# Who makes the low halves of the experts' weights: twelve subtractions moved from GpSimd to VectorE in a hybrid encoder block

## The chip, the cores and the metric

One core of one Trainium2 chip runs the whole block in one launch. The metric is the device time of a launch in microseconds (us). Engines are named as the profile names them: PE is TensorE, PEld its weight loads, DVE is VectorE, ACT is ScalarE, POOL is GpSimd, and SP is SyncE, which here only issues transfers.

## What is computed

The block is an encoder layer on 2048 tokens of 1024 numbers: a projection, differential attention, a Hyena long convolution, a gated merge, and then a mixture of 16 experts in which each expert chooses 256 tokens. Only the last part is touched:

```
g, idx = lax.top_k(aff.transpose(0, 2, 1), cap)
xin = jax.vmap(lambda ub, ib: ub[ib])(u, idx)
hg = jnp.einsum('becd,edf->becf', xin, w_gate)
hu = jnp.einsum('becd,edf->becf', xin, w_up)
eo = jnp.einsum('becf,efd->becd', jax.nn.silu(hg) * hu, w_down)
```

The weighted rows of `eo` are then added back to the tokens they came from.

## The kernel before

**Two-part numbers.** Each float32 operand of a matmul is kept as a high part `hi` (a rounded copy) and a low part `lo`, the operand minus `hi`. A product takes three matmuls: high with high, high with low, low with high. The helper `split` (L40 to L43) has ACT write `hi` (L42) and DVE write `lo` (L43), and it is used all over the kernel.

**The experts.** `moe_phase` handles the experts one after another. For expert e, `hidden(e)` takes eight weight tiles in the order gate 0, up 0, gate 1, up 1 and so on; a tile is 128x2048 numbers, 1 MB. `down(e)` takes four more. Between the two, `turn(e + 1)` transposes the tokens gathered for the next expert on PE (L1554) and splits them. Each weight tile goes through `weight`: a transfer from SP's queue into a buffer `r` (L1504, or L1501 for the down weights; three buffers), then `hi` into `wh` and `lo` into `wl` (four buffers each). So the transfer of a tile waits until the split of the tile three places before it is done, and ACT's copy waits until PE is through with the tile four places before.

**The two kinds of experts.** For the first three experts (`ALONE = 3`) the gate and up matmuls take 256 columns each (L1590); for the others a different arrangement of 512 and 256 columns is used (L1615, L1618). Only for the first three, `weight` is called with `early` for four of the twelve tiles: the up tiles of j = 2 and 3, and the down tiles of j = 1 and 3. There ACT writes `hi` (L1508) and GpSimd, not VectorE, writes `lo` (L1509).

**What else runs there.** While PE works for the first experts, DVE also looks for the 256 best tokens of the following ones: `narrow` for experts 1 and 2 (a search whose counts go through PE, L1310 to L1333, then L1352 to L1377), and `narrow_all` for all the others at once (L1389 to L1405). `onehot` (L1521) and `index` (L1528 on PE, L1533 to L1538 on DVE) turn the result into row numbers, with which GpSimd gathers the tokens by an indirect transfer (L1541). GpSimd also issues the indirect transfers that add an expert's result to the output (L1641). After each group of matmuls `step()` advances this search.

**What sets the order.** Each engine runs its instructions in the order of its own queue. That order is made when the program is built, by a scheduler that places instructions by estimated times, so that a change of engine for one instruction can move others.

Of the kernel before, what the change touches and what calls it, by code (L numbers as in the profile page):

```python
# [9 lines left out]
F32 = mybir.dt.float32  # L10
# [3 lines left out]
AF = mybir.ActivationFunctionType  # L14
ALU = mybir.AluOpType
# [16 lines left out]
def dap(ap, off, dims):  # L32
    return bass.AP(tensor=ap.tensor, offset=ap.offset + off, ap=dims)
# [6 lines left out]
def split(nc, hi, lo, src):  # L40

    nc.scalar.activation(hi, src, AF.Copy)  # L42
    return nc.vector.tensor_tensor(lo, src, hi.bitcast(F32), ALU.subtract)  # L43


def mm3(nc, out, a, b, start, stop):

    nc.tensor.matmul(out, a[0], b[0], start=start, stop=False)  # L48
    nc.tensor.matmul(out, a[0], b[1], start=False, stop=False)  # L49
    return nc.tensor.matmul(out, a[1], b[0], start=False, stop=stop)  # L50
# [1213 lines left out]
ALONE = 3  # L1264
# [214 lines left out]
def moe_phase(E, aff, u2d, wg, wu, wd, out):  # L1479
    nc, tc = E.nc, E.tc  # L1480
    rows = out.rearrange("b l d -> (b l) d")
    with ExitStack() as ctx:
# [9 lines left out]

        READY = {}

        def weight(w, e, j, down, early=False):
            if (w is wu, e, j, down) in READY:
                return READY.pop((w is wu, e, j, down))
            r = pr.tile([128, 2048], F32, name="r")
            if down:
                v = r.rearrange("p (k c) -> p k c", c=1024)  # L1500
                nc.sync.dma_start(v, dap(w, (e * FH + j * 256) * D, [[D, 128], [128 * D, 2], [1, D]]))  # L1501
            else:
                v = r.rearrange("p (k c) -> p k c", c=256)
                nc.sync.dma_start(v, dap(w, e * D * FH + j * 256, [[FH, 128], [128 * FH, KD], [1, 256]]))  # L1504
            hi = pw.tile([128, 2048], F32R, name="wh")
            lo = pw.tile([128, 2048], F32R, name="wl")
            if early:
                nc.scalar.activation(hi, r, AF.Copy)  # L1508
                nc.gpsimd.tensor_tensor(lo, r, hi.bitcast(F32), ALU.subtract)  # L1509
            else:  # L1510
                split(nc, hi, lo, r)
            c = 1024 if down else 256
            return hi.rearrange("p (k c) -> p k c", c=c), lo.rearrange("p (k c) -> p k c", c=c)

# [59 lines left out]
        def hidden(e):  # L1574
            x2 = XT[e]
            hh = ph.tile([128, 8, CAP], F32R, name="hh")
            hl = ph.tile([128, 8, CAP], F32R, name="hl")
            for j in range(4):
                s = po.tile([128, 2, CAP], F32, name="s")
                if e < ALONE:  # L1580
                    ps = []
                    for w in (wg, wu):
                        wt = weight(w, e, j, False, j > 1 and w is wu)
                        p = sg.tile([128, 2, CAP], F32, name="pg")
                        for f in range(2):
                            cs = slice(f * 128, (f + 1) * 128)
                            for a in range(2):
                                for k in range(KD):
                                    for b in range(2 - a):
                                        nc.tensor.matmul(p[:, f], wt[a][:, k, cs], x2[:, k, b], start=a + k + b == 0,  # L1590
                                                         stop=a == 1 and k == KD - 1)
                            step()
                        ps.append(p)
                    nc.scalar.activation(s, ps[0], AF.Silu)
                    nc.vector.tensor_tensor(s, s, ps[1], ALU.mult)
                else:
                    gu = []
                    for w in (wg, wu):
                        wt = weight(w, e, j, False)
                        o = s if w is wg else po.tile([128, 2, CAP], F32, name="su")  # L1600
                        for f in range(2):
                            beside(o[:, f], wt, x2, f)
                            step()
                        gu.append(o)
                    nc.scalar.activation(s, s, AF.Silu)
                    nc.vector.tensor_tensor(s, s, gu[1], ALU.mult)
                split(nc, hh[:, 2 * j:2 * j + 2], hl[:, 2 * j:2 * j + 2], s)
            HT[e] = hh, hl

        def beside(o, wt, x2, f):  # L1610

            p = sg.tile([128, 2, CAP], F32, name="pg")
            cs = slice(f * 128, (f + 1) * 128)
            for k in range(KD):
                nc.tensor.matmul(p.rearrange("p a c -> p (a c)"), wt[0][:, k, cs],  # L1615
                                 x2[:, k].rearrange("p a c -> p (a c)"),
                                 start=k == 0, stop=False, skip_group_check=True)
                nc.tensor.matmul(p[:, 0], wt[1][:, k, cs], x2[:, k, 0],  # L1618
                                 start=False, stop=k == KD - 1, skip_group_check=True)
            nc.scalar.activation(o, p[:, 1], AF.Copy)  # L1620
            nc.vector.tensor_tensor(o, o, p[:, 0], ALU.add)

        def down(e):
            hh, hl = HT[e]
            ix, g, _ = IX[e]
            ys = [sy.tile([128, 512], F32, name="py") for _ in range(4)]
            for j in range(4):
                wt = weight(wd, e, j, True, e < ALONE and j % 2 == 1)
                for f in range(2):
                    k = j * 2 + f  # L1630
                    for s in range(2):
                        for c in range(2):
                            mm3(nc, ys[s * 2 + c], (hh[:, k, s * 128:(s + 1) * 128], hl[:, k, s * 128:(s + 1) * 128]),
                                (wt[0][:, f, c * 512:(c + 1) * 512], wt[1][:, f, c * 512:(c + 1) * 512]),
                                k == 0, k == 7)
                    step()
            for s in range(2):
                y = po.tile([128, D], F32, name="y")
                for c in range(2):
                    nc.scalar.activation(y[:, c * 512:(c + 1) * 512], ys[s * 2 + c], AF.Copy, scale=g[:, s:s + 1])  # L1640
                nc.gpsimd.indirect_dma_start(out=rows, out_offset=bass.IndirectOffsetOnAxis(ap=ix[:, s:s + 1], axis=0),  # L1641
                                             in_=y, in_offset=None, compute_op=ALU.add)
# [16 lines left out]
        def step():  # L1659
            next(ahead, None)  # L1660
            if tick[0] >= 16:
                next(wide, None)
            tick[0] += 1
# [4 lines left out]
        for e in range(NE):  # L1668
            hidden(e)
            if e + 1 < NE:  # L1670
                turn(e + 1)
            down(e)
# [65 lines left out]
```

## Time and profile before

| | us |
|---|---|
| median of 3 runs | 3774.24 (3770.49 to 3776.69) |
| the profiled execution, its time | 3763.67 |
| the profiled execution, its span | 3761.9 |

The span runs from the first to the last instruction that the profiler saw; 1.8 us of the execution's time lie around it. In the trace, times are us from the span's start. A row of the order of time (the timeline) merges equal instructions that follow each other; its first number is the start, its second the time from the first start to the last end, and in brackets stands how long the engine sat idle before it and what ended that. [...]

### The profile page before, as it was taken

To read this page: it belongs to the slowest core of one execution; us is meant where nothing else is said; L and a number is where in the kernel's file an instruction comes from. 1 tells how busy PE (TensorE), PEld (TensorE's weight loads), DVE (VectorE), ACT (ScalarE), POOL (GpSimd) and SP (SyncE) were. 2 spreads that over 40 slices of the span, in tenths; PEclk is the share of its full clock that TensorE was granted. 3 is DMA by queue.
4 is the path that set the end of the run, shared out by engine and by line. 5 is a ranking of instruction groups with operands and counts; after the bars stand their busy time and mean duration, and the time that the engine had idled before them with its cause. 6 is when DMAs were issued, how large, how long until landed. Compare 5 with 4: busy or idle time off the path is not lost. (4 is left out here: it accounts for less than half of the span.)

```text
span 3761.9 us, 55714 instructions
## 1 busy us (share of the span) xinstructions
PE 3621.2 (96%) x21122; PEld 3128.0 (83%) x21122; DVE 2495.9 (66%) x5447; ACT 1819.1 (48%) x2787; POOL 476.8 (13%) x435
## 2 busy tenths in 40 slices
PE   8999999999999999999999799997899999999998
PEld 6788888788888888798999688886888888888887
DVE  8944552698989897167777644558775666665663
ACT  5411111566666675367666432323345555555553
POOL 0000000000000000354453100001330101100100
PEclk9999999999999999999999799998999999999999
DMA  4286774312222222766876853325556766766764
GB/s 156 76 254 165 187 188 129 115 64 84 92 83 93 64 92 71 235 176 211 237 210 202 262 165 129 108 80 168 168 179 192 220 215 205 222 208 206 224 202 123
DMA packets 449713, 607.28 MB, mean 161 GB/s; under 512 B 37467, under 2 KB 333411, under 8 KB 442789
## 3 DMA queue, kind: packets, MB, share of 16 engines
q1 hardware_dynamic: 389301, 438.81, 37.3%
q0 software_dynamic: 34736, 127.16, 12.6%
q10 hardware_dynamic: 25408, 37.76, 2.8%
q8 instruction: 166, 2.72, 0.3%
q14 instruction: 102, 0.84, 0.1%
HBM read 464.16 MB, written 139.46 MB: 160 GB/s over the span
## 5 line engine op out<-in xcount | busy, mean ns | idle before, releaser
L43 DVE TENSOR_TENSOR wl<-r,wh 128x2048 fp32r<-128x2048 f32 (+1 forms) x236 | 449.5, 1910 | 330.9 <-ACT wh L42 330.7
L1615 PE MATMUL pg<-x,wh 128*128 128x512 f32 x1664 | 587.0, 398 | 0.0
L42 ACT ACTIVATE wh<-r 128x2048 fp32r<-128x2048 f32 (+1 forms) x236 | 379.4, 1610 | 356.8 <-PE pg L1615 138.5
L1618 PE MATMUL pg<-x,wl 128*128 128x256 f32 x1664 | 466.3, 280 | 0.0
L1615 PEld LDWEIGHTS pg<-x,wh 128*128 128x128 f32 x1664 | 312.4, 188 | 75.3
L411 DVE TENSOR_SCALAR_CACHE_REDUCE x<-p 128x512 f32<-128x512 f32 x512 | 335.0, 685 | 23.4 <-PE p L410 22.8
L410 PE MATMUL p<-k,qT 128*128 128x512 f32 x1024 | 327.0, 415 | 0.0
L1618 PEld LDWEIGHTS pg<-x,wl 128*128 128x128 f32 x1664 | 314.1, 189 | 0.5
L418 ACT ACTIVATE x<-x,sm 128x2048 f32<-128x2048 f32 x128 | 256.7, 2006 | 45.8 <-DVE sm L415 42.1
L42 ACT ACTIVATE ah<-pt 128x512 fp32r<-128x512 f32 x256 | 150.1, 595 | 151.5 <-PE pt L433 150.9
L49 PE MATMUL py<-wl,hh 128*128 128x512 f32 x512 | 205.3, 401 | 0.0
L48 PE MATMUL p<-wh,uh 128*128 128x512 f32 x512 | 203.5, 398 | 0.4 <-ACT uh L134 0.4
L48 PE MATMUL py<-wh,hh 128*128 128x512 f32 x512 | 203.4, 397 | 0.0
L50 PE MATMUL py<-wh,hl 128*128 128x512 f32 x512 | 202.1, 395 | 0.0
L43 DVE TENSOR_TENSOR bl<-p,bh 128x512 fp32r<-128x512 f32 x192 | 124.7, 685 | 115.7 <-ACT bh L42 114.6
L43 DVE TENSOR_TENSOR al<-pt,ah 128x512 fp32r<-128x512 f32 x256 | 174.9, 685 | 38.8 <-ACT ah L42 37.5
L50 PE MATMUL p<-wh,ul 128*128 128x512 f32 x512 | 200.4, 392 | 0.0
L49 PE MATMUL p<-wl,uh 128*128 128x512 f32 x512 | 200.3, 392 | 0.0
L410 PEld LDWEIGHTS p<-k,qT 128*128 128x128 f32 x1024 | 171.4, 190 | 24.3 <-ACT qT L368 2.8
L1641 POOL DMA_INDIRECT out_dram<-y,ix x32 | 71.7, 2242 | 752.1 <-ACT y L1640 648.6
L433 PE MATMUL pt<-idf,x 128*128 128x128 f32 x1024 | 164.7, 272 | 0.0
L48 PE MATMUL gp<-gh,gu 128*128 128x512 f32 x384 | 157.1, 409 | 3.7 <-ACT go L294 2.4
(435 smaller groups left out, 9504.0 us busy)
## 6 DMA issues: line engine op xcount, KB each, us to landing
r<-in_w_gate SPq DMA_DIRECT2D x64, 1024.0 KB, 5.1
r<-in_w_up SPq DMA_DIRECT2D x64, 1024.0 KB, 5.7
r<-in_w_down SPq DMA_DIRECT2D x64, 1024.0 KB, 5.8
gu<-s_ud POOLq DMA_DIRECT2D x48, 1024.0 KB, 6.0
tg<-in_tg POOLq DMA_DIRECT2D x68, 384.0 KB, 4.1
xt<-in_x SPq DMA_DIRECT2D x32, 512.0 KB, 5.0
s_filt<-fo SPq DMA_DIRECT2D x128, 128.0 KB, 3.2
zr<-s_filt SPq DMA_DIRECT2D x64, 256.0 KB, 3.2
```

Of the source, the lines that this page charges most:

```text
L42: nc.scalar.activation(hi, src, AF.Copy)
L43: return nc.vector.tensor_tensor(lo, src, hi.bitcast(F32), ALU.subtract)
L48: nc.tensor.matmul(out, a[0], b[0], start=start, stop=False)
L49: nc.tensor.matmul(out, a[0], b[1], start=False, stop=False)
L50: return nc.tensor.matmul(out, a[1], b[0], start=False, stop=stop)
L410: nc.tensor.matmul(p, qT[:, t * 2 + m, a], k2[:, m, o:o + 512], start=a == 0, stop=a == 1)
L411: nc.vector.tensor_scalar(x[:, o:o + 512], p, 0.125, None, ALU.mult, ALU.max, accum_out=sm[:, c * 2 + i:c * 2 + i + 1])
L418: nc.scalar.activation(x, x, AF.Exp, bias=sm[:, 8 + m:9 + m], accum_out=acc)
L433: nc.tensor.transpose(p[:, i, t * 128:(t + 1) * 128], EX[u, t, 0][:, (g * 2 + i) * 128:(g * 2 + i + 1) * 128], E.idf)
L1615: nc.tensor.matmul(p.rearrange("p a c -> p (a c)"), wt[0][:, k, cs], x2[:, k].rearrange("p a c -> p (a c)"), start=k == 0, stop=False, ski ...
L1618: nc.tensor.matmul(p[:, 0], wt[1][:, k, cs], x2[:, k, 0], start=False, stop=k == KD - 1, skip_group_check=True)
L1641: nc.gpsimd.indirect_dma_start(out=rows, out_offset=bass.IndirectOffsetOnAxis(ap=ix[:, s:s + 1], axis=0), in_=y, in_offset=None, compute_o ...
```

## The change

`weight` loses its parameter `early`; every weight tile goes through `split`. Twelve subtractions, four for each of the first three experts, leave GpSimd's queue and stand in VectorE's.

```
-        def weight(w, e, j, down, early=False):
+        def weight(w, e, j, down):
...
-            if early:
-                nc.scalar.activation(hi, r, AF.Copy)
-                nc.gpsimd.tensor_tensor(lo, r, hi.bitcast(F32), ALU.subtract)
-            else:
-                split(nc, hi, lo, r)
+            split(nc, hi, lo, r)
...
-                        wt = weight(w, e, j, False, j > 1 and w is wu)
+                        wt = weight(w, e, j, False)
...
-                wt = weight(wd, e, j, True, e < ALONE and j % 2 == 1)
+                wt = weight(wd, e, j, True)
```

Lines behind L1507 have a number lower by 4 in the changed kernel: L1590 is L1586 there, L1595 is L1591, L1541 is L1537, L1641 is L1637. The scheduler also moves other instructions. Three places show how.

POOL, from the gather for the first expert on, before:

```order
L1541 DMA xg<-s_u,ix 128x1024 x2
L1509 TENSOR_TENSOR wl<-r,wh 128x2048 x2
L1541 DMA xg<-s_u,ix 128x1024 x2
L1509 TENSOR_TENSOR wl<-r,wh 128x2048 x2
L1641 DMA out_dram<-y,ix 2048x1024
L1541 DMA xg<-s_u,ix 128x1024 x2
L1641 DMA out_dram<-y,ix 2048x1024
L1509 TENSOR_TENSOR wl<-r,wh 128x2048 x4
```

POOL at the same place, now:

```order
L1537 DMA xg<-s_u,ix 128x1024 x4
L1637 DMA out_dram<-y,ix 2048x1024 x2
L1537 DMA xg<-s_u,ix 128x1024 x2
L1637 DMA out_dram<-y,ix 2048x1024 x2
L1537 DMA xg<-s_u,ix 128x1024 x2
```

Only the issues of indirect transfers are left in this queue (`xg` are gathered tokens, `y` an expert's result).

DVE, in the search for the tokens of expert 1, while PE works on the gate and up tiles of expert 0 (`cnt`, `k`, `thr`, `ti`, `run` belong to the search; `wl` is a weight tile's low part), before:

```order
L1314 TENSOR_REDUCE cnt<-ge 128x15 x2
L1324 TENSOR_SCALAR k<-pt 128x15
L1333 SCALAR_TENSOR_TENSOR ti<-k,thr 128x1
L1352 TENSOR_TENSOR ti<-ti 128x1
L1356 TENSOR_SCALAR run_26318<-aff,ti 128x16
L1357 TENSOR_SCALAR run_26318<-aff,ti 128x16
L1359 COPY flag<-run_26318 128x32
```

DVE at the same place, now:

```order
L1314 TENSOR_REDUCE cnt<-ge 128x15 x2
L43 TENSOR_TENSOR wl<-r,wh 128x2048
L1324 TENSOR_SCALAR k<-pt 128x15
L1591 TENSOR_TENSOR s<-s,pg 128x512
L1333 SCALAR_TENSOR_TENSOR ti<-k,thr 128x1
L43 TENSOR_TENSOR wl<-r,wh 128x2048
L1352 TENSOR_TENSOR ti<-ti 128x1
L43 TENSOR_TENSOR hl<-s,hh 128x512
L1356 TENSOR_SCALAR run_26318<-aff,ti 128x16
L1357 TENSOR_SCALAR run_26318<-aff,ti 128x16
L1359 COPY flag<-run_26318 128x32
```

Two weight tiles' low parts and two pieces of the hidden activations (`s`, `hl`) now stand inside the search.

PE at that place (L1317 is the matmul that sums `cnt`, L1365 the first that needs `run`), before:

```order
L1590 MATMUL pg<-x_26262,wl 128x256 x7
L1317 LDWEIGHTS onesb
L1317 MATMUL pt<-cnt,onesb 128x15
L1590 MATMUL pg<-x_26262,wl 128x256
L1590 MATMUL pg<-x_26262,wh 128x256 x15
L1365 LDWEIGHTS onesb
L1365 MATMUL pt<-run_26318,onesb 128x1
```

PE at the same place, now:

```order
L1586 MATMUL pg<-x_26262,wl 128x256
L1317 LDWEIGHTS onesb
L1317 MATMUL pt<-cnt,onesb 128x15
L1586 MATMUL pg<-x_26262,wl 128x256 x7
L1586 MATMUL pg<-x_26262,wh 128x256 x16
L1586 MATMUL pg<-x_26262,wl 128x256 x8
L1586 MATMUL pg<-x_26262,wh 128x256 x16
L1586 MATMUL pg<-x_26262,wl 128x256 x8
L1586 MATMUL pg<-x_26262,wh 128x256 x6
L1365 LDWEIGHTS onesb
L1365 MATMUL pt<-run_26318,onesb 128x1
```

Between the two small matmuls stood 16 of the expert's; now there are 61.

## Rows read from the trace of the kernel before

**Rows 1.** The page: span of the profiled execution.

```profile
span 3761.9 us, 55714 instructions
```

**Rows 2.** Windows: length, busy us of PE, PEld, DVE, ACT, POOL, PEclk, DMA share, GB/s.

```profile
2600.00:2840.00 240.00, 213.75 (x1478) 195.04 (x1477) 179.42 (x410) 85.48 (x76) 74.20 (x22) 0.94 0.54 171
2900.00:3000.00 100.00, 100.00 (x556) 85.11 (x555) 59.53 (x71) 52.53 (x61) 10.57 (x6) 1.00 0.68 207
```

**Rows 3.** The order of time on PE, 2600 to 2840: its idle times.

```profile
2607.30 0.17 PE L1317 MATMUL pt<-cnt,onesb 128*128 128x15 bf16 x1 [3.70 <-DVE cnt L1314]
2618.30 0.20 PE L1528 MATMUL pt<-val,oh 128*128 128x5 bf16 x2 [3.22 <-DVE oh L1521]
2641.39 0.16 PE L1317 MATMUL pt<-cnt,onesb 128*128 128x3 bf16 x1 [3.72 <-DVE cnt L1314]
2659.07 0.66 PE L1554 MATMUL pt<-idf,xg 128*128 128x128 f32 x4 [3.95 <-DVE x L43]
...
2703.10 0.38 PE L1394 MATMUL pt<-wcnt,same 128*128 128x3 f32 x2 [1.25 <-DVE junk L1389]
2716.08 0.39 PE L1394 MATMUL pt<-wcnt,same 128*128 128x3 f32 x2 [0.77 <-DVE junk L1389]
2729.54 0.39 PE L1394 MATMUL pt<-wcnt,same 128*128 128x3 f32 x2 [1.24 <-DVE junk L1389]
...
2743.53 1.12 PE L1554 MATMUL pt<-idf,xg 128*128 128x128 f32 x4 [4.09 <-DVE x L43]
2822.42 0.66 PE L1554 MATMUL pt<-idf,xg 128*128 128x128 f32 x4 [3.90 <-DVE x L43]
```

**Rows 4.** The order of time on DVE, the same stretch.

```profile
2597.92 0.17 DVE L1327 SCALAR_TENSOR_TENSOR cand<-k,base 128x15 f32<-128x15 f32 x1
...
2598.07 0.68 DVE L43 TENSOR_TENSOR hl<-s,hh 128x512 fp32r<-128x512 f32 x1
...
2599.44 2.28 DVE L43 TENSOR_TENSOR wl<-r,wh 128x2048 fp32r<-128x2048 f32 x1
...
2601.85 4.32 DVE L1327 SCALAR_TENSOR_TENSOR cand<-k,base 128x15 f32<-128x15 f32 x1
...
2635.92 3.98 DVE L1333 SCALAR_TENSOR_TENSOR t<-k,thr 128x1 f32<-128x1 f32 x1
...
2817.15 4.61 DVE L43 TENSOR_TENSOR hl<-s,hh 128x512 fp32r<-128x512 f32 x1 [0.80 <-ACT hh L42]
```

**Rows 5.** The order of time on POOL, the same stretch.

```profile
2599.75 6.39 POOL L1509 TENSOR_TENSOR wl<-r,wh 128x2048 fp32r<-128x2048 f32 x1 [25.65 <-ACT wh L1508]
...
2635.34 4.54 POOL L1509 TENSOR_TENSOR wl<-r,wh 128x2048 fp32r<-128x2048 f32 x1 [5.49 <-ACT wh L1508]
...
2816.68 4.54 POOL L1509 TENSOR_TENSOR wl<-r,wh 128x2048 fp32r<-128x2048 f32 x1 [6.89 <-ACT wh L1508]
```

**Rows 6.** Groups of POOL's instructions: count, busy us, mean ns, idle before.

```profile
L1509 POOL TENSOR_TENSOR wl<-r,wh 128x2048 fp32r<-128x2048 f32 x12 | 57.0, 4751 | 99.8 <-ACT wh L1508 97.9 <-DVE wthr L1405 1.9
```

**Rows 7.** The order of time on PE at two granted clocks.

```profile
2643.60 1.91 PE L1590 MATMUL pg<-x,wl 128*128 128x256 f32 x8
...
2647.67 1.12 PE L1590 MATMUL pg<-x,wl 128*128 128x256 f32 x8
2648.63 0.18 PE L1317 MATMUL pt<-cnt,onesb 128*128 128x15 bf16 x1
```

**Rows 8.** The order of time on ACT: a copy that waited for its load.

```profile
2611.37 1.91 ACT L1508 ACTIVATE wh<-r 128x2048 fp32r<-128x2048 f32 x1 [6.28 <-DMA r<-in_w_up]
```

**Rows 9.** Transfers, 2575 to 2850: totals, then issues with median us to landing.

```profile
DMA packets 33093, 47.46 MB, mean 173 GB/s; under 512 B 816, under 2 KB 28464, under 8 KB 33074
...
r<-in_w_up SPq DMA_DIRECT2D x14, 1024.0 KB, 5.2
```

**Rows 10.** The order of time on POOL: two gathers.

```profile
2685.52 0.99 POOL L1541 DMA_INDIRECT xg<-s_u,ix  x1 [0.30 <-DVE junk L1389]
2686.81 2.84 POOL L1541 DMA_INDIRECT xg<-s_u,ix  x1 [0.30 <-issue]
```

## The prediction

> **What bounds the kernel now.** I read the windows first. Over the stretch of the first three experts, 2600 to 2840 us, PE is busy 213.75 of 240 us at a mean granted clock of 0.94; later, from 2900 to 3000, it is busy all the time at 1.00, with DVE at 60% and the transfers at 207 GB/s [rows 2]. So the end of the kernel is set by PE alone, and a microsecond that PE loses before 2840 is a microsecond of the span of 3761.9 us [rows 1]. The stretch has 26.25 us in which PE does nothing, and a further price in clock.
>
> The second view is the order of time on PE. Nine idle times make 25.84 of those 26.25 us (3.70, 3.22, 3.72, 3.95, 1.25, 0.77, 1.24, 4.09, 3.90), and every one was ended by DVE: by the counts of the search, the one-hot rows, or the low part of the turned tokens [rows 3]. So the question is why DVE was late. It was not short of time as such: it is busy 179 of 240 us.
>
> The third view, the order of time on DVE, answers that. The same kind of instruction that takes 0.17 us at 2597.92 takes 4.32 us at 2601.85; a piece of hidden activation takes 0.68 us at 2598.07 and 4.61 at 2817.15 [rows 4]. There are twelve such long rows in the stretch, the shortest 3.98 us. The fourth view, the order of time on POOL, shows twelve subtractions L1509, 57.0 us in all [rows 5, 6]. They match one to one, and a pair ends together: POOL's first runs from 2599.75 to 2606.14 and DVE's long row ends at 2606.17; POOL's at 2635.34 ends at 2639.88, DVE's at 2639.90 [rows 4, 5]. POOL's first row is itself 6.39 instead of 4.54 us long, and the 1.85 us of difference are nearly the 1.97 us for which DVE's subtraction, begun at 2599.44, still ran. So the two engines do not do these things side by side: whichever comes second stands still until the first is done. A subtraction on POOL costs DVE some 4 us, in place of the 2.28 us that it takes on DVE [rows 4].
>
> **The change, part by part.**
>
> *Twelve subtractions leave POOL.* DVE's twelve long rows go back to their own lengths of 0.2 to 0.7 us: about 12 x 4.0 = 48 us of DVE time. With them go the idle times of PE that they made, 25.8 us.
>
> *The clock.* After an idle time PE restarts at half clock: at 2643.60 eight matmuls took 1.91 us, at 2647.67 the same eight 1.12 us [rows 7]. A mean of 0.94 over 240 us is 14.4 us of full-speed work lost (13.2 to 15.6 by the rounding of the row). Some of the low clock falls into the idle time itself, where it costs nothing, so I take 13. Bounds: 0 if the clock falls for another reason, 15.6 if all of it comes back.
>
> *Twelve subtractions come to DVE.* 12 x 2.28 = 27.4 us. DVE's work in the stretch becomes 179.4 - 48 + 27.4 = 159 us, in a stretch that shrinks to about 204 us: 78%, after 75% now. It is more room than it looks, since DVE serves its queue in order and no row holds it for 4 us any more. In the later stretch DVE makes every low part by itself and PE never waits [rows 2].
>
> *The new order.* What can go wrong is a subtraction that stands in front of a row that PE needs. I take the place shown above. Behind the count DVE now has two weight subtractions, two rows of 0.68 and some ten short rows of 0.17: 4.56 + 1.36 + 1.7 = 7.6 us. PE has 61 matmuls there, and at 0.12 us each (eight from 2647.67 to 2648.63 [rows 7]) they cover 7.3 us, where the 16 before would have covered 1.9. The wait left is 0.3 us. That holds if the weights are there. The second of those two subtractions is the eighth tile's; its load starts when the fifth tile's low part is done, 2601.72 [rows 4], lands 5.2 us later [rows 9], and ACT's copy of 1.91 us [rows 8] has it ready at 2608.8. DVE gets there after two subtractions, ten short rows and one of 0.68, at 2608.7. So that row is in time, but with nothing to spare. For all twelve I take 12 x 0.25 = 3 us of new waits; the bounds are 0 and 27.4 us, if every added subtraction came between PE and what it waits for.
>
> *The other queues.* SP's loads lose a wait: a buffer `r` that POOL released after 4.5 us or more is released by DVE after 2.28. POOL's gathers and scatters no longer queue behind subtractions. An added subtraction on DVE can still stretch one of them: a gather's issue took 2.84 us at 2686.81 beside a DVE subtraction, the one before it 0.99 [rows 10]. I cost this at nothing, because the tokens are gathered long before PE turns them; without that cover it would be 1.9 us for each expert. ACT's copies stay as they are, L42 in place of L1508.
>
> *The loads.* The stretch moves 47.46 MB in 275 us, 173 GB/s [rows 9]. With 36 us less that is 199 GB/s, below the 207 that the later stretch sustains with PE never waiting [rows 2]. So the loads do not take the gain back.
>
> *The sum.* 25.8 + 13 - 3 = 36 us. The profiled execution took 3763.67 us, its span and 1.8 us around it; it would take 3727.7. The median of the runs shown is 10.6 us above it, so I take the 36 us off the median of 3774.24: **3738 us**, 0.95% faster. A measurement of this kernel can tell about 0.2%, 7.5 us, from no change.
>
> **The rivals.**
>
> *The clock dips at the transposes anyway.* Three of the six long idle times come right before transposes (L1554) [rows 3], so these rows cannot tell whether the wait or the transposes let the clock fall there. If it was the transposes, about half of the 13 us stays: 25.8 + 6.5 - 3 = 29 us, 3745. Against it: at the restart after the first and the third idle time the rows are ordinary matmuls, and the clock was low there too [rows 7]. Chance 0.06. [...]
>
> *Part of it comes back.* The idle times go, but some of the added subtractions stand in PE's way, and the clock falls at these places. For it: the eighth tile above has no slack. With no gain in clock and 6 us of new waits it is 25.8 - 6 = 20 us: 3754. Against it: the order was made anew with the rows in it. Chance 0.11.
>
> *PE is not the only bound.* If the loads or ACT's copies held the stretch to its present length, the idle times would only move: 3774. Against it stand the 173 GB/s, under what the later stretch moves, and ACT busy 85 of 240 us. For it, one copy waited 6.28 us for its load [rows 8]. Chance 0.04.
>
> *Slower: the wait moves into DVE's queue.* POOL now sits 97.9 us waiting for ACT's copies before its twelve rows [rows 6], and nobody minds, since nothing that PE needs stands behind them. If the order puts the added rows too early, DVE takes this wait, with the search, the one-hots and the turned tokens behind it. The place is each of the twelve rows in the first three experts. It decides from (25.8 + 13) / 12 = 3.2 us of PE's time for each row; with 5 us, still below the 6.28 us that ACT's copy waited [rows 8], it is 60 - 39 = 21 us slower: 3795. Against it: at the place that I followed the row comes when its weights do. A second way to the slower side: if the long rows on DVE had another cause than POOL, the 27.4 us would only be added, 3802; the common ends speak against that. [...] Chance 0.05.
>
> *The change doesn't do what it says.* In POOL's order no subtraction is left, so this is excluded.
>
> **How the numbers follow.** The forecast has 0.74. Its own range is 30 to 41 us of gain, 41 being the whole idle time and the upper bound of the clock: 3733 to 3744. The range given must leave out no more than 2 in 10, so it takes in the first two rivals and some microseconds between executions: 3728 to 3755. Faster by over 0.2%: the forecast and the first two rivals, exactly 0.91; same: the third rival and a little of the fourth, 0.05; slower: the rest of the fourth, 0.04.
>
> **What would show it.** In the profile of the changed kernel no L1509 is left on POOL; no small DVE row in that stretch lasts over 1 us; the rows of the twelve additional L43 take 2.28 us; PE's idle time from 2600 to the start of the fourth expert falls from 26 to under 5 us, and the mean clock there rises to 0.98 or more; the fourth expert starts some 36 us earlier and everything behind it is unchanged. I am wrong if PE's idle times come back under other names: "DVE wl L43", or a search row whose DVE predecessor waited for ACT's copy.

## The result, and the profile after

The changed kernel takes **3735.26 us** (median of 4 runs, 3732.43 to 3740.06), the kernel before, run beside it on the same chip, 3775.47 (4 runs, 3770.49 to 3777.73). The ratio is 0.9897, 95% interval 0.9879 to 0.9914: 32 to 46 us faster, 40 between the medians. The forecast was 3738. The execution that was profiled took 3733.82 us.

The page of the changed kernel, beside [rows 1]:

```profile
span 3732.0 us, 55713 instructions
```

Its windows (columns as in [rows 2]; the first row answers to the first there, the second to the later stretch):

```profile
2600.00:2840.00 240.00, 238.62 (x1732) 217.18 (x1732) 182.38 (x477) 107.89 (x99) 20.52 (x14) 1.00 0.65 207
...
2900.00:3000.00 100.00, 100.00 (x599) 85.74 (x598) 66.85 (x104) 53.39 (x65) 7.79 (x6) 1.00 0.68 215
```

In the same 240 us PE now does 1732 matmuls where it did 1478, is busy 238.62 us where it was 213.75, and its granted clock (PEclk, as a share of the full one) is 1.00 where it was 0.94 [rows 2]. The order of time on PE, 2600 to 2815, has four rows with more than 0.1 us of idle time left, where before there were the nine of [rows 3] and one of 0.21 us:

```profile
2621.08 0.16 PE L1365 MATMUL pt<-run,onesb 128*128 128x1 bf16 x1 [0.19 <-DVE run L1361]
...
2670.72 0.35 PE L1394 MATMUL pt<-wcnt,same 128*128 128x3 f32 x2 [0.34 <-DVE junk L1389]
...
2692.18 0.38 PE L1394 MATMUL pt<-wcnt,same 128*128 128x3 f32 x2 [0.26 <-DVE junk L1389]
...
2699.74 0.39 PE L1394 MATMUL pt<-wcnt,same 128*128 128x3 f32 x2 [0.27 <-DVE junk L1389]
```

They sum to 1.06 us, against 25.84 for the nine. The turns, which cost 3.95, 4.09 and 3.90, have none. The order of time on DVE shows why: the small row that took 4.32 us takes 0.17 again, the piece of hidden activation that took 4.61 takes 0.68 (compare [rows 4]).

```profile
2605.61 0.17 DVE L1327 SCALAR_TENSOR_TENSOR cand<-k,base 128x15 f32<-128x15 f32 x1
...
2605.76 0.68 DVE L43 TENSOR_TENSOR hl<-s,hh 128x512 fp32r<-128x512 f32 x1
...
2616.85 2.29 DVE L43 TENSOR_TENSOR wl<-r,wh 128x2048 fp32r<-128x2048 f32 x1 [0.71 <-ACT wh L42]
```

The last row is the low part of the eighth tile, one of the twelve that came from GpSimd; it has a short wait for ACT's copy before it.

To compare the stretch itself, I take it from the first weight load for a gate or up matmul of the first expert to the first one of the fourth expert, and from there to the last one of the last expert:

| us | before | changed | difference |
|---|---|---|---|
| first three experts | 2581.4 to 2844.5, 263.1 | 2589.1 to 2814.6, 225.5 | -37.6 |
| fourth expert on | 2844.5 to 3724.4, 879.9 | 2814.6 to 3694.4, 879.8 | -0.1 |

The windows of the first row, before and then now:

```profile
2581.40:2844.50 263.10, 236.84 (x1640) 217.22 (x1639) 197.97 (x448) 97.30 (x86) 74.44 (x22) 0.94 0.55 172
```

```profile
2589.10:2814.60 225.50, 224.12 (x1642) 206.00 (x1641) 176.20 (x460) 97.21 (x86) 14.69 (x11) 0.99 0.63 201
```

PE's idle time falls from 26.3 to 1.4 us, and its busy time for the same matmuls by 12.7 (a record or two are missing).

In this execution the first expert started 7.7 us later than in that of before, in a part that the change leaves alone (every engine runs its instructions in the same order there); in the profiled executions of the first five experiments, which leave that part alone too, the start lies anywhere from 2582.1 to 2601.5. That is why the two spans differ by 29.9 us only. The gain itself is all in the stretch.

### The profile page after: what moved, and what is told of

It is laid out like the page before. It is cut to its first block, busy times and chain, and to the rows that moved or that the text cites. A ratio compares the mean times of both kernels' runs of the same rounds, so it can differ in the third digit from the quotient of the medians.

```text
span 3732.0 us, 55713 instructions
## 1 busy us (share of the span) xinstructions
PE 3610.1 (97%) x21122; PEld 3118.8 (84%) x21122; DVE 2473.9 (66%) x5459; ACT 1820.0 (49%) x2787; POOL 415.3 (11%) x423
## 5 line engine op out<-in xcount | busy, mean ns | idle before, releaser
L43 DVE TENSOR_TENSOR wl<-r,wh 128x2048 fp32r<-128x2048 f32 (+1 forms) x248 | 477.0, 1928 | 333.5 <-ACT wh L42 333.3
L42 ACT ACTIVATE wh<-r 128x2048 fp32r<-128x2048 f32 (+1 forms) x248 | 402.3, 1624 | 379.7 <-PE pg L1611 138.4
L1637 POOL DMA_INDIRECT out_dram<-y,ix x32 | 70.4, 2199 | 807.2 <-ACT y L1636 698.4
```

## Experiments

**The two halves of the change.** In the kernel before, only the down tiles' subtractions go to DVE (`hidden_pool`), or only the up tiles' (`down_pool`).

```
-                wt = weight(wd, e, j, True, e < ALONE and j % 2 == 1)
+                wt = weight(wd, e, j, True)
```

> Half of the change: the six low parts of down tiles go to VectorE, the six of up tiles stay on GpSimd. Theory (a GpSimd subtraction holds VectorE up for 4 us, and PE stands idle where something that it needs waits behind): the idle times that go with the up tiles' rows stay, 3.70 + 3.22 + 1.25 + 0.77 = 8.9 us, with about 6 us of clock behind them; so some 15 us above the changed kernel's 3735, near 3750. Rival (the low part itself came too late from GpSimd, 4.6 us in place of 2.3): PE has no idle time before a weight's low part in either kernel, so both halves would be worth nothing and the gain would come from the new order alone, 3735 or 3775. Rival (transposes let the clock fall anyway): the clock dips at the turns stay here though the down tiles are on VectorE.

```
-                        wt = weight(w, e, j, False, j > 1 and w is wu)
+                        wt = weight(w, e, j, False)
```

> The other half: the six low parts of up tiles go to VectorE, the six of down tiles stay on GpSimd. Theory: the idle times that go with the down tiles' rows stay, 3.72 + 3.95 + 1.24 + 4.09 + 3.90 = 16.9 us, with about 7 us of clock behind them; some 24 us above the changed kernel, near 3759, and the two halves together make the whole, 40 us. Rivals: as for the other half, 3735 or 3775; if the transposes let the clock fall, the dips are the same in both halves.

Measured: `hidden_pool` 3750.69 us (ratio to before 0.9942, 0.9921 to 0.9964), stretch 241.2 us; `down_pool` 3754.37 (0.9944, 0.9922 to 0.9966), stretch 244.4 us. The first has the forecast time, the second is a little better than that. Their gains, 22 and 21 us by the ratios, make 43 together, the whole change 39; each is uncertain by some 8 us. The order of time on PE shows that each half has its own waits. In `hidden_pool` the long ones are in the search and the one-hot rows, none before a transpose:

```profile
2607.83 0.17 PE L1317 MATMUL pt<-cnt,onesb 128*128 128x15 bf16 x1 [3.70 <-DVE cnt L1314]
...
2618.89 0.20 PE L1528 MATMUL pt<-val,oh 128*128 128x5 bf16 x2 [3.27 <-DVE oh L1521]
```

In `down_pool` the longest stand before two turns and at one place of the search (two of 1.25 and 1.47 us stand at other places of it):

```profile
2651.17 0.17 PE L1317 MATMUL pt<-cnt,onesb 128*128 128x15 bf16 x1 [4.16 <-DVE cnt L1314]
...
2735.86 0.66 PE L1554 MATMUL pt<-idf,xg 128*128 128x128 f32 x4 [4.09 <-DVE x L43]
...
2814.09 0.66 PE L1554 MATMUL pt<-idf,xg 128*128 128x128 f32 x4 [3.90 <-DVE x L43]
```

So the subtractions of the hidden part delayed the search, and those of the down part the turns and, here and there, the search. The clock follows the waits and not the transposes: in `hidden_pool` it is 1.00 over all three turns,

```profile
2645.00:2823.00 178.00, 175.15 (x1236) 158.50 (x1235) 136.49 (x326) 76.06 (x68) 34.79 (x12) 1.00 0.61 190
```

while in `down_pool` matmuls of 512 columns take 0.63 us soon after the two waits before turns (from 2737.16 and 2815.57 on), where they otherwise take 0.39.

**Is it GpSimd's reading?** The theory says that GpSimd holds DVE up while it reads. The rivals say that the low parts came late from it (4.6 us in place of 2.28), that its buffers came free late, or that the order of the queues was worse. So I leave the changed kernel as it is, and give GpSimd twelve instructions whose result nobody uses, at the places of the old ones. A copy of one column on ACT makes each wait for the tile's high part.

```
+        jk = pc.tile([128, 2048], F32, name="jk")
+        nc.vector.memset(jk, 0.0)
...
+            if e < ALONE and (j % 2 == 1 if down else j > 1 and w is wu):
+                nc.scalar.activation(jk[:, 0:1], hi[:, 0:1].bitcast(F32), AF.Copy)
+                nc.gpsimd.tensor_tensor(jk, jk, jk, ALU.subtract)
```

In `junk_two_reads` it is the subtraction shown; in `junk_no_read` the last line is `nc.gpsimd.memset(jk, 0.0)`, in `junk_one_read` it is `nc.gpsimd.tensor_copy(jk, jk)`.

> The changed kernel, and beside each of the twelve moved subtractions GpSimd does a useless one on a tile of its own (two inputs in SBUF, 128x2048), started by a one-column copy on ACT. Nobody waits for it, and no weight buffer is held by it. Theory (the two engines exclude each other): VectorE's long rows of 4 us are back, twelve of them, while VectorE also has its 27 us of subtractions; the whole gain is lost and some more, 3775 to 3800. Rivals (the low parts were late; the weight buffers were released late; the order was worse): none of these is touched, so it stays at 3735.

> The same, but GpSimd's useless instruction only writes (a memset of 128x2048). Theory in its narrow form (it is the reading of two inputs that excludes): no long rows on VectorE, 3735 to 3740. In a wide form (any GpSimd instruction on SBUF excludes VectorE): long rows as long as the memset lasts, and a loss in proportion. Rivals: 3735.

> The changed kernel with a useless GpSimd copy (one input, 128x2048, in place) beside each of the twelve subtractions. Theory: a single stream of reads is enough to exclude VectorE's second input; VectorE gets twelve rows as long as the copy lasts. The copy should last between the memset's 1.81 us and the subtraction's 3.60, say 2.4; that is 12 x 2 = 24 us of VectorE's time, which its free time takes up in part: 3737 to 3755. If only instructions with two inputs exclude, no long rows and 3736.

Measured:

| | us | ratio to before | stretch, us | mean of the `hl` rows on DVE, ns |
|---|---|---|---|---|
| `junk_two_reads` | 3772.06 | 0.9993 (0.9983 to 1.0003) | 259.6 | 2016 |
| `junk_one_read` | 3746.56 | 0.9929 (0.9912 to 0.9945) | 234.2 | 1586 |
| `junk_no_read` | 3736.30 | 0.9898 (0.9872 to 0.9923) | 225.9 | 753 |

The last column is from the groups by line on DVE in each kernel's own stretch, twelve rows each; without any such instruction, in the changed kernel, it is 684. PE, ACT and DVE run their instructions in the same order in the three kernels, so a different order of the queues is no cause of what sets them apart. GpSimd's groups in the three kernels (count, then busy us and mean ns of one, then idle time before):

```profile
L1513 POOL TENSOR_TENSOR jk<-jk 128x2048 f32<-128x2048 f32 x12 | 55.1, 4592 | 110.4 <-ACT jk L1512 110.3
```

```profile
L1513 POOL COPY jk<-jk 128x2048 f32<-128x2048 f32 x12 | 32.8, 2735 | 107.5 <-ACT jk L1512 107.5
```

```profile
L1513 POOL MEMSET jk<- 128x2048 f32 x12 | 21.8, 1813 | 109.6 <-ACT jk L1512 109.6
```

The subtractions in `junk_two_reads` give nothing to anyone, free no buffer that another waits for, and take back 36 of the 39 us (by the ratios: 0.9993 against 0.9897). By the stretch it is 34 of 38. The three rivals would have had it near 3735; they fall. The median lies 3 us under the range that I expected. A row of its DVE and the row of POOL beside it:

```profile
2621.12 3.96 DVE L43 TENSOR_TENSOR hl<-s,hh 128x512 fp32r<-128x512 f32 x1
```

```profile
2620.93 3.60 POOL L1513 TENSOR_TENSOR jk<-jk 128x2048 f32<-128x2048 f32 x1 [27.59 <-ACT jk L1512]
```

POOL's ends at 2624.53, DVE's at 2625.08, so 0.55 us are left of DVE's own 0.68: it did nearly all of its work when POOL was through. Twelve instructions of nearly the same kind that read nothing, in `junk_no_read`, cost nothing that can be measured. Beside the memsets DVE's subtractions of weight tiles still take 2.28 or 2.29 us, beside two of the copies 2.67 and 2.75 (the mean of 38 goes from 2288 to 2308 ns). The one-input copy costs 0.32% or 12 us (8.7 in the stretch) and makes PE idle for 0.9 to 1.8 us at six places. So on these three kernels it is the reading, and one stream of it is enough: the mean `hl` row takes 2016 ns beside two inputs, 1586 beside one, 753 beside none. Why the two hold each other up, these runs do not show. One row makes the whole difference of 753 from 684; it is shown at the end.

**The same offload for all experts.** If GpSimd's subtractions cost so much in three experts, the kernel before with 64 of them, in all sixteen, should show it in thirteen experts more.

```
-                        wt = weight(w, e, j, False)
+                        wt = weight(w, e, j, False, j > 1 and w is wu)
...
-                wt = weight(wd, e, j, True, e < ALONE and j % 2 == 1)
+                wt = weight(wd, e, j, True, j % 2 == 1)
```

> The kernel before, with the same four tiles of every expert on GpSimd and not of the first three alone: 64 subtractions in place of 12. Theory: what a held-up VectorE row costs depends on what waits behind it. Experts 4 to 16 have no search, so only the turn to the next expert (an idle time of about 4 us and 2 us of clock) is at risk: up to 13 x 6 = 78 us above before, 3774 to 3852; VectorE is 60% busy there, and 52 x (4 - 2.3) = 88 us more work would fit. Rival (a held-up row always costs PE its length): 52 x 4 = 208 us, 3982.

Measured: 3913.51 us, ratio 1.0373 (1.0351 to 1.0395). The part from the fourth expert on takes 1017.5 us instead of 879.9, 10.6 us more for each of the 13 experts; I had expected 6 at most, so this is a miss on the low side; the rival, with 208 us, is too high by about as much. The windows of that part, in `pool_all_experts` and then in the changed kernel:

```profile
2852.00:3868.00 1016.00, 923.09 (x5047) 777.63 (x5047) 638.62 (x679) 467.30 (x557) 313.46 (x101) 0.96 0.59 182
```

```profile
2815.00:3694.00 879.00, 879.00 (x5051) 752.03 (x5050) 549.71 (x731) 472.01 (x558) 85.31 (x50) 1.00 0.68 211
```

DVE is busy 63% of the time in the first and also 63% in the second, so its share of busy time says nothing here. PE is idle for 92.9 us, and at a clock of 0.96 it is busy 44.1 us longer with the same matmuls (923.09 against 879.00; a few records are missing), together the 137 us between the two windows. What PE waited for there:

```profile
PE pt L1554 <- DVE x L43: 52.7, 24, 2.8
PE pg L1615 <- DVE su L1621: 35.1, 11, 3.2
```

I had counted one wait for each turn. There are two at each of the twelve turns, and a second kind beside them: PE also waits for the sums L1621 that DVE makes from a finished product, before the next product may start (L1615). At the turn that I followed, at 2988 to 2994, only the second wait has a held row before it (L1606, 3.82 us beside POOL's 4.59); what makes the first was not followed up.

**Is the same move good in the Hyena stage?** There, too, GpSimd makes low parts: 164 subtractions of 128x512 (L721). I gave all of them to DVE in the changed kernel (`hyena_dve`), then only the 96 for `zl` (`hyena_z_dve`) and only the 68 for `yl` (`hyena_y_dve`).

```
             def split_pool(hi, lo, src):
-                nc.scalar.activation(hi, src, AF.Copy)
-                nc.gpsimd.tensor_tensor(lo, src, hi.bitcast(F32), ALU.subtract)
+                split(nc, hi, lo, src)
```

> The changed kernel, and the other 164 GpSimd subtractions (of 128x512, in the Hyena convolution) also go to VectorE, so that GpSimd makes no low part anywhere. A try for a version that beats both. Theory: in that stage VectorE is some 75% busy and most of its rows read PSUM and are not held up; only 5 to 10 us of PE's idle time there are ended by these GpSimd rows. 164 x 0.69 = 113 us more on VectorE in some 500 us would bring it to 90% and more: a loss of 5 to 30 us against the changed kernel, 3740 to 3765. Rival (GpSimd always costs VectorE more than it saves): a gain of 5 to 10 us, 3725 to 3730.

> The changed kernel, with the 96 subtractions for zl of the Hyena stage (128x512) made by DVE, the 68 for yl left on GpSimd. Theory of adding up (each subtraction moved costs the same, 35 us over 164 of them): 96 x 0.21 = 20 us slower than the changed kernel, 3756 us. Rival (only when both groups are moved does DVE's queue make ACT's high parts late, PE's wait for ACT bh of 22.6 us): within 5 us of the changed kernel, 3731 to 3741 us. Second rival (the 177 us that POOL waited before these rows were holding PE's operands up, and DVE is held by POOL at some of them): faster than the changed kernel, under 3730 us.

> The changed kernel, with the 68 subtractions for yl of the Hyena stage made by DVE, the 96 for zl left on GpSimd. Theory of adding up: 68 x 0.21 = 14 us slower than the changed kernel, 3750 us. Rival (only both together): within 5 us, 3731 to 3741 us. Second rival (DVE is better at it alone): under 3730 us.

Measured: `hyena_dve` 3770.57 us (ratio to before 0.9990, 0.9979 to 1.0001), `hyena_z_dve` 3759.65 (0.9968, 0.9958 to 0.9979), `hyena_y_dve` 3744.19 (0.9925, 0.9898 to 0.9951). By the ratios they are 35, 27 and 11 us slower than the changed kernel: the whole move loses more than I expected, and its two parts add up to it within the noise, as the first theory of the last two runs has it. The 11 us of `yl` alone are not clear of noise by the ratios, whose intervals overlap. The loss lies in the stage: from the first row for `zl` to the last `z<-z,g` it takes 611.4 to 621.0 us in the eight kernels that leave it alone, and 652.1, 637.7 and 624.5 in these three. So here GpSimd earns its keep. The rows show what the offload costs DVE. The groups on DVE, 1530 to 2100, in the changed kernel:

```profile
L43 DVE TENSOR_TENSOR bl<-p,bh 128x512 fp32r<-128x512 f32 x192 | 125.0, 686 | 117.0 <-ACT bh L42 115.9
L851 DVE TENSOR_TENSOR ya<-ya,sp 128x256 f32<-128x256 f32 x68 | 54.5, 801 | 0.0
L847 DVE TENSOR_TENSOR ya<-p,sp 128x512 f32<-128x512 f32 x68 | 46.6, 686 | 20.4 <-PE p L50 16.9 <-POOL yl L721 3.0 <-issue 0.2
```

and in `hyena_dve`, where L850 is the line that is L851 above:

```profile
L43 DVE TENSOR_TENSOR bl<-p,bh 128x512 fp32r<-128x512 f32 x192 | 124.7, 682 | 66.2 <-ACT bh L42 65.3
...
L850 DVE TENSOR_TENSOR ya<-ya,sp 128x256 f32<-128x256 f32 x62 | 25.7, 415 | 0.0
```

Most of DVE's rows there have one operand from a matmul's result (`p`), and they take 686 ns with GpSimd at work and 682 without. Of those with both operands in SBUF, L851 is held up: 801 against 415 ns, 68 x 0.39 = 26 us in all. The others lose little or nothing: `vl` has 729 against 685 ns, L892 447 against 423. The 164 subtractions would take DVE 164 x 0.68 = 112 us. So there the offload costs DVE a quarter of what it saves; in the experts it cost 4.0 us for each 2.28. What PE then waits for is in the chain ACT to PE: the wait for the high parts `bh` is 2.5 us in the changed kernel, and in `hyena_z_dve`:

```profile
PE p L48 <- ACT bh L42: 20.1, 10, 4.3
```

Why ACT makes these later is not settled. DVE is busy 411 of the 570 us in `hyena_dve`, so it isn't simply full; in the changed kernel it was 374, or 66%, not the 75% on which I had based my expectation. And in all three kernels PE, ACT and DVE run this stage in a new order, so the load on DVE and the order are not told apart here.

No version that I ran beats the changed kernel; its stretch of the first three experts has about 1 us of idle time left to gain.

## Why the prediction was right

**PE is the bound, and the time comes out of the stretch.** Right: 37.6 us there, nothing behind it. The rival that PE is not the only bound falls.

**The two engines do not read side by side.** Right, and now shown by experiment rather than by common ends alone: `junk_two_reads` brings the cost back without any of the change's other effects (3772.06 us, `hl` rows of 2016 ns in the mean), `junk_no_read` does not (3736.30 us, 753 ns). It is shown for rows of DVE with all operands in SBUF; those with one operand from a matmul's result take 686 ns in the Hyena stage with GpSimd at work and 682 without. With it falls the second way to the slower side, another cause of the long rows.

**25.8 us of idle time.** Right: 25.84 became 1.06. That is all that there is of new waits, for which I had taken 3 us with bounds of 0 and 27.4, from one place stretched to twelve. The wait at L1365 was forecast as 0.3 us and is 0.19. The eighth tile's low part, said to be "in time, with nothing to spare", waited 0.71 us for ACT's copy, and at most the 0.19 at L1365 of that reached PE. So the rival "the wait moves into DVE's queue" had only a little in it. DVE's waits for ACT's copies in the stretch (total, times, longest), in the kernel before, 2581.4 to 2844.5, and then in the changed one, 2589.1 to 2814.6:

```profile
DVE wl L43 <- ACT wh L42: 15.7, 8, 3.1
```

```profile
DVE wl L43 <- ACT wh L42: 17.7, 13, 3.1
```

Of the 97.9 us that POOL had waited [rows 6], DVE took over 2.0, in five more waits, and none of it reached PE beyond the 1.06 us. "Part of it comes back" falls by the same rows.

**13 us of clock.** Right: PE's busy time for the same matmuls fell by 12.7 us, and that with the 24.9 of idle time makes the 37.6. "After an idle time" was too wide, though: in the trace of before, a granted clock of 0.50 to 0.53 (in windows of 2 us) follows the six idle times of 3.2 us and more, while after 1.25 us, at 2703.34, sixteen matmuls take 2.16 us, with the clock at 1.00. The clock now reads 1.00 through the three turns of the stretch (2650 to 2662, 2722 to 2732, 2794 to 2806), so the transposes do not lower it in this kernel when they come without a wait, and the first rival falls here. That is shown for transposes that stand four at a time (0.60 to 0.66 us) between matmuls.

**DVE's room.** 78% busy was forecast, and it is 176.20 of 225.50 us in the stretch, 78% (197.97 of 263.10 before, 75%): 21.8 us less work, where 48 - 27.4 = 20.6 were forecast. **The loads** were forecast at 199 GB/s and run at 201 there (172 before).

**What did not read as forecast.** I wrote that the fourth expert would start "some 36 us earlier"; in the profiled execution it starts 29.9 earlier, because the start of the first expert moves by up to 19 us between executions. A stretch with its own start and end was the thing to name. Of the gathers, one issue beside DVE's subtractions took 2.36 us (0.94 undisturbed), as bounded, and nobody waited for it.

## What to carry to other kernels

In this kernel VectorE paid for work given to GpSimd where its row had all operands in SBUF and GpSimd read SBUF too (the `hl` rows took 2016 ns in the mean beside a subtraction, 684 with nothing beside them). So put the time that VectorE's rows are held beside the time that it saves, row by row, before calling it an offload; 4.0 us against 2.28 was a loss, 26 against 112 a gain. Look too at what stands behind the row: here 48 us of held rows went with 37.6 us of PE's time, idle or at half clock, while the 27.4 us of subtractions that took their place left it 1.06 us of waits. The sign of a held row here was that it was far longer than its like and ended together with, or just after, a GpSimd row (3.96 us for 0.68, its end 0.55 us after POOL's); the share of busy time hid it (63% from the fourth expert on, with held rows and without), since a held row counts as busy. And judge a change by the stretch between two events of its own, not by the time since the start.

## What was not expected of the hardware

A subtraction on GpSimd whose inputs and output are one and the same tile took 3.60 us at its shortest, against 4.54 with three tiles [rows 5], and a copy 1.89, hardly more than the 1.81 of a memset of that size. Nor was a memset free at every place. In `junk_no_read` the fifth of the twelve ran from 2684.08 to 2685.90, and these rows of DVE all end at 2685.94 or just before:

```profile
2683.90 2.04 DVE L1397 TENSOR_SCALAR wbase<-steps,wthr 128x3 f32<-128x3 f32 x1
2684.03 1.90 DVE L1389 TENSOR_SCALAR_CACHE_REDUCE junk<-top,wcand 128x256 bf16<-128x256 f32 x1
...
2684.43 1.51 DVE L43 TENSOR_TENSOR hl<-s,hh 128x512 fp32r<-128x512 f32 x1
```

The first is a row of 3 numbers per partition with a column of scalars. In the changed kernel the longest of its kind is 0.23 us, in the kernel before 4.27. At the same place the copy of `junk_one_read` and the subtraction of `junk_two_reads` go with a row of L1397 of 2.12 and 3.85 us. So VectorE instructions with a single tensor operand were held up as well (2.04 us for 0.23, 1.90 for 0.48), here, it seems, beside an instruction that only writes. It is one hold among twelve, too short to be seen in the time; which of DVE's instructions began it was not tried apart.
